# Seven products instead of eight for five of eight k-pairs of an MLP's up-projection, token-major, with the residual stream in DRAM

## The chip, the cores and the metric

The kernel runs on one core of one Trainium2 chip. The metric is the device time of one execution in microseconds, the median over several runs. The core has a matmul engine (TensorE, PE in the profile, with its weight loads as PEld), a vector engine (VectorE, DVE), an activation engine (ScalarE, ACT), a general engine (GpSimd, POOL) and a sync engine (SyncE, SP) that here only issues transfers. Operands lie in SBUF, matmul results in PSUM, which has eight banks of 128 x 512 fp32; weights, inputs and outputs lie in DRAM.

## The reference

Two layers over 256 tokens of width 2048, all in fp32. Each layer is a mixer (layer 0: gated short convolution and chunked attention; layer 1: two gated linear recurrences) and an MLP, each between two RMS norms and added to the stream h. Cut to what matters here:

```python
for l in range(DEPTH):                       # 2
    g = norm_g[l]
    u = rmsnorm(h, g[0])
    y = mixer_l(u) @ w_out[l]                # w_out 2048 x 2048
    h = h + rmsnorm(y, g[1])
    u = rmsnorm(h, g[2])
    z = jnp.square(jax.nn.relu(u @ mlp_w1[l])) @ mlp_w2[l]   # 2048 -> 8192 -> 2048
    h = h + rmsnorm(z, g[3])
```

## The kernel before

**Precision.** TensorE multiplies in a reduced fp32 format (F32R). To get fp32 accuracy, every operand is split into a high part (ScalarE's cast, `whi`, L222) and a residual (VectorE's subtraction, `wlo`, L223), and a product is three matmuls: high x high, high x residual, residual x high.

**Weights.** A *slab* is two k-tiles of 128 rows by 512 columns (512 KB). SyncE's queue brings it into one of 7 raw tiles, ScalarE and VectorE convert it into one of 6 pairs of tiles `whi`, `wlo`, TensorE uses it. Each weight is used once, by both token tiles (two times 128 tokens).

**Forms of a block of 512 output columns.** `Block` (L235 to L237) is token-major: for each token tile 128 columns of x are the stationary operand and the weights stream through, 512 at a time; a slab is 12 matmuls. `UpBlock` (L271, L274) is feature-major: 128 columns of weights are stationary and x streams through, 512 columns wide (both parts of both token tiles) for the high weights and 256 wide for the residual; a slab is 8 + 8 matmuls. Its result already has hidden features on partitions, as the next product needs it.

**The MLP.** The hidden width 8192 is cut into 8 chunks of 1024. `mlp` runs up(0), then for c = 1 to 7 up(c) and down(c-1), then down(7). An up chunk is 16 slabs: two `UpBlock`s of 512 columns, only the first block of chunk 0 is a `Block`. Its evacuation (L452 to L462) joins the halves, squares the ReLU and splits the result into `hid[c]`. A down chunk is 4 `Block`s of 4 slabs, added into `y` (L476).

**What sets the order.** The program is written slab by slab (`run`), and a scheduler lays the instructions of each engine out in one fixed order; each engine then works through its order and waits on semaphores. Weight conversions are placed some slabs ahead, as far as the tiles allow. The last four slabs of the out-projection and of the MLP are done for the first token tile, then for the second, with the norm between (`tail`, `between`); the next phase then begins with 6 slabs for the first token tile only (`lead`). `later` puts an action off by a number of slabs.

**The stream.** h (two tiles of 128 x 2048) and y stay in SBUF through the out-projection and the MLP; h goes to DRAM (`hsave`) only for layer 1's mixer. x is loaded into h at the start, and the sums of squares are taken from there.

Of the kernel before, what the change touches and what calls it, by code (L numbers as in the profile page):

```python
# [11 lines left out]
F32 = mybir.dt.float32  # L12
# [15 lines left out]
X_BUFS = 1  # L28
# [11 lines left out]
def trunk(ctx, tc, x, x_t, norm_g, ng_cols, e_win, rbf, e_wout, o_win, lbraw, smalls, wa2, ba, o_wout, w1, w2,  # L40
# [160 lines left out]

    class Block:
# [7 lines left out]
        def load(self, s, extra=None):  # L210
            k0 = self.kts[s * SLAB]
            raw = rawp.tile([P, SLAB, 512], F32, name="raw")
            pool, tag, bufs = (wp, "w", W_BUFS) if extra is None else (extra, "x", X_BUFS)
            hi = pool.tile([P, SLAB, 512], F32R, name=tag + "hi", bufs=bufs)
            lo = pool.tile([P, SLAB, 512], F32R, name=tag + "lo", bufs=bufs)
# [66 lines left out]

    def banks():
        return [accp.tile([P, 512], F32, name="acc") if j % 2 == 0 else aux() for j in range(4)]
# [34 lines left out]
    def run(blocks, tail=0, between=None, extra=None, rate=0.0, hooks={}, lead=None):  # L319
# [24 lines left out]
        for t in range(NT):  # L344
            for i, (b, s) in enumerate(items[n:]):
                if t == 0:
                    b.load(s, extra if i < X_BUFS else None)
                b.mm(s, t)
            if between is not None and t == 0:
                between(0)  # L350
# [34 lines left out]
    def gbc_tile(pool, l, i):  # L385
        t = pool.tile([P, D], F32, name="gbc", bufs=1)

        def load(c):
            def f():
                cs = slice(c * 1024, (c + 1) * 1024)  # L390
                nc.sync.dma_start(out=t[:, cs], in_=norm_g[l, i, cs].partition_broadcast(P))
            return f
        return t, [load(0), load(1)]


    def out_proj(l, w, kts, X2, y, h, X, ypool, reload=()):
        gbc, gl = gbc_tile(ypool, l, 1)
        hooks = {2: gl[0:1], 5: gl[1:2]}
        for i, f in enumerate(reload):
            hooks[9 + 2 * i] = [f]  # L400
# [11 lines left out]
        def between(t):  # L412
            add_post(t, y, rsqrt_of(total(ss[t]), 1, 1.0 / D), h)
            rst[t] = prenorm(t, h[t], l, 2, X, ypool)

        run([Block(wview(w), nb * 512, 512, kts if nb == 0 else ALLK, X2.get, mk(nb)) for nb in range(4)],
            tail=TAIL, between=between, extra=ypool, hooks=hooks)
        return rst, lambda: between(1)

    def mlp(l, X, rst, y, ypool, between, lead):  # L420
        gbc, gl = gbc_tile(ypool, l, 3)
# [7 lines left out]
        def finish(t):  # L429
            between(t, rsqrt_of(sl[t], 1, None, base[t]))  # L430
# [6 lines left out]
        def up(c):  # L437
            def mk(j):
                def evac(t, ps):
                    r = ypool.tile([P, 512], F32, name="relu", bufs=2)  # L440
                    nc.scalar.activation(out=r, in_=ps, func=AF.Relu)
                    r2 = ypool.tile([P, 512], F32, name="ulo", bufs=2)
# [4 lines left out]
            def mk_up(j):  # L447
                st2 = {}

                def evac(i, ps):  # L450
                    a = ypool.tile([P, 256], F32, name="ulo", bufs=2)
                    nc.scalar.copy(out=a, in_=ps[:, 256:512])  # L452
                    if i % 2 == 0:
                        st2["z"] = ypool.tile([P, 2, 256], F32, name="relu", bufs=2)
                    z = st2["z"]
                    nc.vector.tensor_tensor(out=z[:, i % 2, :], in0=ps[:, 0:256], in1=a, op=ALU.add)  # L456
                    if i % 2:
                        r2 = ypool.tile([P, 2, 256], F32, name="relu2", bufs=1)
                        nc.vector.scalar_tensor_tensor(out=r2, in0=z, scalar=0.0, in1=z, op0=ALU.max, op1=ALU.mult)
                        hi, lo = pair(x2p, "x2", 2, 256)  # L460
                        nc.scalar.copy(out=hi, in_=r2)
                        nc.vector.tensor_tensor(out=lo, in0=r2, in1=hi, op=ALU.subtract)  # L462
                        hid[c].put2(c * 8 + j * 4 + i - 1, hi, lo)
                return evac
            hid[c] = Hid()
            return [Block(w1v, (c * 2 + j) * 512, 512, ALLK, X.get, mk(j)) if c == 0 and j == 0 else
# [604 lines left out]
```

## Time and profile before

| | |
|---|---|
| median of 3 runs | 2280.32 us (2279.87 to 2280.66) |
| the profiled execution | 2280.16 us |
| its span in the trace | 2278.2 us |
| PE, PEld busy | 2262.2 us, 1915.0 us |
| DVE, ACT, POOL busy | 1415.3 us, 1089.8 us, 15.2 us |
| read from HBM, written | 424.28 MB, 4.20 MB |
| mean granted clock of TensorE | 0.998 |

Busy time is the time in which an engine had at least one instruction running; matmuls overlap, so a busy TensorE need not be at its peak. In a group row stand line, engine, operation, result <- inputs, shapes and count, then busy us and mean ns of one, then the idle time before them and what ended it. In a timeline row stand start, duration, engine, line and operation, and in brackets the idle time just before and what ended it.

### The profile page before, as it was taken

The page shows a single profiled execution, that of the slowest core. Times are in us where ns is not written, and L with a number is a line of the kernel's source. Part 1 is how long each engine was busy: PE and PEld are TensorE (multiplying, and loading weights), DVE is VectorE, ACT ScalarE, POOL GpSimd, SP SyncE. Part 2 cuts the span into 40 slices and gives each one's busy share as a digit, 9 for nine tenths or more (in the row PEclk, how much of TensorE's full clock was granted, in tenths as well). Part 3 has the DMA queues.
Part 4 walks back from the last instruction along what each step waited for, and adds up shares of the span by engine and source line. Part 5 has one row for each costly group of instructions (what it writes and reads, how often), then busy time and mean ns, then how long its engine had stood idle before and what let it go on. Part 6 is the DMA issues. An engine that isn't in the chain of part 4 may idle for free.

```text
span 2278.2 us, 29937 instructions
## 1 busy us (share of the span) xinstructions
PE 2262.2 (99%) x11486; PEld 1915.0 (84%) x11486; DVE 1415.3 (62%) x1856; ACT 1089.8 (48%) x1550; POOL 15.2 (1%) x30
## 2 busy tenths in 40 slices
PE   9999999999999999999999999999999999999998
PEld 7888888888888888888888888888888888888886
DVE  6656656655565665656877767657556565556556
ACT  7444445544444444444746454546444444444443
POOL 0000000000000000000000000000000000000000
PEclk9999999999999999999999999999999999999999
DMA  9555565655655656656655445475565665665652
GB/s 345 167 177 174 168 229 176 206 188 189 194 188 192 193 187 192 192 187 203 213 174 167 153 144 159 166 257 185 186 193 187 193 193 185 192 191 191 194 187 100
DMA packets 219390, 430.43 MB, mean 189 GB/s; under 512 B 13392, under 2 KB 14192, under 8 KB 218992
## 3 DMA queue, kind: packets, MB, share of 16 engines
q1 hardware_dynamic: 217152, 422.63, 58.0%
q0 software_dynamic: 1376, 4.79, 0.7%
q8 instruction: 90, 1.47, 0.3%
q10 hardware_dynamic: 720, 1.11, 0.1%
q14 instruction: 52, 0.43, 0.1%
HBM read 424.28 MB, written 4.20 MB: 188 GB/s over the span
## 4 chain that ended last, share of the span: by engine, by line
PE 97%; ACT 1%; DVE 1%; DMA 1%; issue 0%; SPq 0%; DVEq 0%; ACTq 0%
PE aux L274 23%; PE acc L235 18%; PE acc L236 18%; PE acc L237 18%; PE aux L271 12%; PE acc L274 3%; PE acc L271 2%; PE aux L815 1%; PE aux L175 1%; DMA h<-x 1%; PE aux L862 0%; ACT junk L362 0%; DVE wlo L223 0%; PE aux L700 0%; DMA raw<-e_win 0%
## 5 line engine op out<-in xcount | busy, mean ns | idle before, releaser
L223 DVE TENSOR_TENSOR wlo<-raw,whi 128x1024 fp32r<-128x1024 f32 (+1 forms) x781 | 952.9, 1223 | 760.7 <-ACT whi L222 759.3
L222 ACT CAST whi<-raw 128x1024 fp32r<-128x1024 f32 (+1 forms) x781 | 821.5, 1054 | 1029.9 <-PE acc L237 590.0
L274 PE MATMUL aux<-xt,whi 128*128 128x512 f32 x2240 | 590.4, 393 | 0.0
L235 PE MATMUL acc<-whi,x 128*128 128x512 f32 x1264 | 492.7, 390 | 0.0
L236 PE MATMUL acc<-wlo,x 128*128 128x512 f32 x1264 | 492.3, 389 | 0.0
L237 PE MATMUL acc<-whi,x 128*128 128x512 f32 x1264 | 492.0, 389 | 0.0
L274 PEld LDWEIGHTS aux<-xt,whi 128*128 128x128 f32 x2240 | 401.8, 189 | 75.5 <-DVE relu L456 4.2
L271 PE MATMUL aux<-xt,wlo 128*128 128x256 f32 x2240 | 339.4, 282 | 0.0
L271 PEld LDWEIGHTS aux<-xt,wlo 128*128 128x128 f32 x2240 | 317.8, 190 | 23.1
L237 PEld LDWEIGHTS acc<-whi,x 128*128 128x128 f32 x1264 | 237.3, 188 | 49.3
L235 PEld LDWEIGHTS acc<-whi,x 128*128 128x128 f32 x1264 | 237.3, 188 | 48.7
L236 PEld LDWEIGHTS acc<-wlo,x 128*128 128x128 f32 x1264 | 237.3, 188 | 48.5
L235 PE MATMUL acc<-whi,xt 128*128 128x512 f32 x576 | 227.8, 398 | 1.8 <-ACT xt L522 1.5
L236 PE MATMUL acc<-wlo,xt 128*128 128x512 f32 x576 | 225.5, 392 | 1.9 <-DVE wlo L223 1.8
L237 PE MATMUL acc<-whi,xt 128*128 128x512 f32 x576 | 225.2, 391 | 0.0
L236 PEld LDWEIGHTS acc<-wlo,xt 128*128 128x128 f32 x576 | 108.3, 188 | 25.4 <-DVE wlo L223 4.3
L235 PEld LDWEIGHTS acc<-whi,xt 128*128 128x128 f32 x576 | 108.0, 188 | 24.6 <-ACT xt L522 2.0
L237 PEld LDWEIGHTS acc<-whi,xt 128*128 128x128 f32 x576 | 108.1, 188 | 22.8 <-issue 0.3
L274 PE MATMUL acc<-xt,whi 128*128 128x512 f32 x320 | 101.5, 398 | 0.0
L271 PE MATMUL acc<-xt,wlo 128*128 128x256 f32 x320 | 63.9, 281 | 0.0
L271 PEld LDWEIGHTS acc<-xt,wlo 128*128 128x128 f32 x320 | 55.6, 189 | 7.2
L476 DVE TENSOR_TENSOR y<-acc,y 128x512 f32<-128x512 f32 x96 | 61.5, 682 | 0.0
(204 smaller groups left out, 1073.7 us busy)
## 6 DMA issues: line engine op xcount, KB each, us to landing
raw<-w SPq DMA_DIRECT2D x512, 512.0 KB, 3.7
raw<-o_win SPq DMA_DIRECT2D x112, 512.0 KB, 3.7
raw<-e_win SPq DMA_DIRECT2D x95, 512.0 KB, 4.2
raw<-e_wout SPq DMA_DIRECT2D x32, 512.0 KB, 4.4
raw<-o_wout SPq DMA_DIRECT2D x32, 512.0 KB, 3.7
gbc<-norm_g SPq DMA_DIRECT2D x8, 512.0 KB, 6.6
h<-x SPq DMA_DIRECT2D x4, 512.0 KB, 12.0
hsave<-h POOLq DMA_DIRECT2D x2, 1024.0 KB, 4.8
```

The costliest lines, as they stand in the source:

```text
L175: nc.tensor.transpose(out=ps[:, k * P:(k + 1) * P], in_=src[:, k * P:(k + 1) * P], identity=ident)
L222: nc.scalar.copy(out=hi[:, a:b, n], in_=raw[:, a:b, n])
L223: nc.vector.tensor_tensor(out=lo[:, a:b, n], in0=raw[:, a:b, n], in1=hi[:, a:b, n], op=ALU.subtract)
L235: nc.tensor.matmul(ps, xh, hi[:, i, 0:self.n], start=first, stop=False)
L236: nc.tensor.matmul(ps, xh, lo[:, i, 0:self.n], start=False, stop=False)
L237: nc.tensor.matmul(ps, xl, hi[:, i, 0:self.n], start=False, stop=last)
L271: nc.tensor.matmul(self.ps[j][:, 0:NT * P], lo[:, i, cs], x[:, 0, :], start=False, stop=last and i == SLAB - 1)
L274: nc.tensor.matmul(self.ps[j], hi[:, i, cs], x, start=s == 0 and i == 0, stop=False)
L476: nc.vector.tensor_tensor(out=y[t][:, cs], in0=ps, in1=y[t][:, cs], op=ALU.add)
L815: nc.tensor.matmul(ps[0:m, u * 64:(u + 1) * 64].rearrange("p (b n) -> p b n", n=wd), K[:, u * P:u * P + m], Q[:, us].rearrange("p (b two n ...
```

## The change

**Pairs.** For chunks 1 to 7 both column halves (L and R, 512 columns each) of an up chunk are computed together, token-major, by `Pairs`, in 8 slabs of one k-pair (two k-tiles by 1024 columns: two raw tiles). For a k-pair the token tiles (a, b), the two k-tiles and the column halves make a 2 x 2 by 2 x 2 block product. `PAIRS = "CSCSSCSS"`: the three C pairs do it plainly, by 8 products (24 matmuls); the five S pairs by 7 products of block sums (21 matmuls), in a form of Strassen's and Winograd's. The sums of x (`Differences`) are made once a layer, the sums of weights in place in the raw tiles. Products of all pairs accumulate in 8 banks (`p2`, `bR`, `p1`; `q3`, `q4`, `q5`, `p6`, `p7`), all PSUM has, and are put together once, behind the last pair (`comb`). A C slab takes two converted tile pairs, an S slab four.

**Token-major results.** The 4 blocks of 128 x 512 are squared, then transposed on TensorE (four 128 x 128 each) and split, some slabs into the following down chunk. Chunk 0 is now two `Block`s, with transposes too.

**The stream.** h now lies in 4 KB half rows (`Row`) in a pool of 7 that it shares with the norm's gains, `Differences` and the scratch U. After the out-projection's norm it is stored to `mid` in DRAM by GpSimd's queue, and read back in the last chunk. In layer 0 the out-projection reads x again; at the start x passes through raw tiles for its sums of squares only. The extra weight tile of the tail (`X_BUFS`) goes. The last output's pieces are 512, 512, 512, 256, 256 columns instead of 256, 512, 512, 512, 256.

```diff
-X_BUFS = 1
+PAIRS = "CSCSSCSS"
...
+    class Differences:
+        def make(self, tmp):
+            p = self.p
+            x = self.X.full[p // 2][:, 2 * (p % 2):2 * (p % 2) + 2, :, :]
+            xf = tmp().rearrange("p (k n) -> p k n", k=2)
+            nc.vector.tensor_tensor(out=xf, in0=x[:, :, 0, :], in1=x[:, :, 1, :], op=ALU.add)
+            a, b = slice(0, P), slice(P, 2 * P)
+            sf = tmp().rearrange("p (i n) -> p i n", i=4)
+            for i, (u, v, op) in enumerate(((xf[:, 0, b], xf[:, 1, b], ALU.subtract),
+                                            (sf[:, 0, :], xf[:, 0, a], ALU.subtract),
+                                            (xf[:, 0, a], xf[:, 0, b], ALU.subtract),
+                                            (sf[:, 1, :], xf[:, 1, a], ALU.add))):
+                nc.vector.tensor_tensor(out=sf[:, i, :], in0=u, in1=v, op=op)
+            o = self.pool.tile([P, 2, 4, P], F32R, name="s")
+            self.hi, self.lo = o[:, 0], o[:, 1]
+            nc.scalar.copy(out=self.hi, in_=sf)
+            nc.vector.tensor_tensor(out=self.lo, in0=sf, in1=self.hi, op=ALU.subtract)
...
+    class Pairs:
+        def load(self, s):
+            raws = [rawp.tile([P, SLAB, 512], F32, name="raw") for _ in range(2)]
+            for raw, n in zip(raws, (self.n0, self.n0 + 512)):
+                nc.sync.dma_start(out=raw, in_=self.wv[:, 2 * s:2 * s + 2, n:n + 512])
+
+            def conv(raw, i=slice(0, SLAB)):
+                hi, lo = w_pair()
+                nc.scalar.copy(out=hi[:, i, :], in_=raw[:, i, :])
+                nc.vector.tensor_tensor(out=lo[:, i, :], in0=raw[:, i, :], in1=hi[:, i, :], op=ALU.subtract)
+                return hi, lo
...
+            L, R = raws
+            if PAIRS[s] == "C":
+                self.w[s] = [conv(L), conv(R)]
+                return
+            plain = conv(L)
+            r1 = conv(R, slice(1, 2))
+            add(R[:, 1, :], R[:, 1, :], R[:, 0, :])
+            add(R[:, 0, :], R[:, 0, :], L[:, 0, :])
+            two = conv(R)
+            add(L[:, 0, :], L[:, 0, :], R[:, 1, :])
+            add(L[:, 1, :], L[:, 1, :], L[:, 0, :])
+            self.w[s] = [plain, r1, two, conv(L)]
+
+        def product(self, n, s, x, w, i):
...
+            nc.tensor.matmul(ps, xh, hi[:, i, :], start=first, stop=False)
+            nc.tensor.matmul(ps, xh, lo[:, i, :], start=False, stop=False)
+            nc.tensor.matmul(ps, xl, hi[:, i, :], start=False, stop=done and not (n == "bR" and i == 0))
+
+        def mm(self, s, t):
...
+            if PAIRS[s] == "C":
+                for n, t, j in (("p2", 0, 0), ("bR", 1, 1), ("q4", 1, 0), ("q3", 0, 1)):
+                    for i in range(2):
+                        self.product(n, s, x[t][i], w[j], i)
+                if "C" not in PAIRS[s + 1:]:
+                    nc.scalar.copy(out=self.U[3], in_=z.pop("bR"))
+                return
...
+            self.product("p1", s, x[0][0], L, 0)
+            if end:
+                nc.scalar.copy(out=s1, in_=z["p1"])
+            self.product("p2", s, x[0][1], L, 1)
+            if end:
+                comb("aL", z["p2"], s1, ALU.add)
+                self.evac(0, 0, out["aL"])
+            self.product("q3", s, d.get(3), r1, 1)
+            self.product("q5", s, d.get(0), two, 0)
+            self.product("p7", s, d.get(2), two, 1)
+            self.product("p6", s, d.get(1), four, 0)
+            if end:
+                nc.vector.tensor_tensor(out=u, in0=z["p6"], in1=s1, op=ALU.add)
+                nc.vector.tensor_tensor(out=u3, in0=z["p7"], in1=u, op=ALU.add)
+            self.product("q4", s, x[1][1], four, 1)
+            if end:
+                comb("aR", z["q5"], u, ALU.subtract)
+                comb("aR", z["q3"], out["aR"], ALU.add)
+                self.evac(0, 1, out["aR"])
+                comb("bL", z["q4"], u3, ALU.add)
+                self.evac(1, 0, out["bL"])
+                comb("bR", z["q5"], u3, ALU.subtract)
+                comb("bR", zb, out["bR"], ALU.add)
+                self.evac(1, 1, out["bR"])
...
-            return [Block(w1v, (c * 2 + j) * 512, 512, ALLK, X.get, mk(j)) if c == 0 and j == 0 else
-                    UpBlock(w1v, (c * 2 + j) * 512, 512, ALLK, X.both, mk_up(j)) for j in range(2)]
+            if c == 0:
+                return [Block(w1v, j * 512, 512, ALLK, X.get, mk(j)) for j in range(2)]
+            n = [0]
+
+            def evac(t, j, z):
+                nc.vector.scalar_tensor_tensor(out=z, in0=z, scalar=0.0, in1=z, op0=ALU.max, op1=ALU.mult)
+                n[0] += 1
+                later(lambda: hid[c].put(t, c * 2 + j, split4(x2p, "x2", transpose4(z))), 2 + 2 * n[0])
+            evac.tile = lambda: ypool.tile([P, 512], F32, name="ulo", bufs=4)
+            return [Pairs(w1v, c * 1024, X, diffs, U, evac)]
...
+        work = [lambda p=p: difference(p) for p in range(len(PAIRS)) if PAIRS[p] == "S"]
+        run(up(0), lead=lead_in, hooks={LEAD + 1 + 2 * i: [f] for i, f in enumerate(work)})
+        scratch()
...
     def load_x(t, i):
-        c = slice(i * 1024, (i + 1) * 1024)
-        nc.sync.dma_start(out=h[t][:, c], in_=x[t * P:(t + 1) * P, c])
+        xp = raw_tile()
+        nc.sync.dma_start(out=xp.rearrange("p a b -> p (a b)"), in_=x[t * P:(t + 1) * P, i * 1024:(i + 1) * 1024])
+        for k in range(2):
+            junk = mp.tile([P, 512], F32, name="junk", bufs=1)
+            nc.scalar.activation(out=junk, in_=xp[:, k, :], func=AF.Square,
+                                 accum_out=xss[t][:, 2 * i + k:2 * i + k + 1])
```

**How the order moves.** Line numbers below are those of the kernel named. First VectorE before, at the turn from an up chunk (the last tiles of `UpBlock`) to the down chunk:

```order
L223 TENSOR_TENSOR wlo_5166<-raw_5164,whi_5165 128x1024
L456 TENSOR_TENSOR relu_5056<-aux_4890,ulo_5054 128x256
L456 TENSOR_TENSOR relu_5056<-aux_4891,ulo_5060 128x256
L459 SCALAR_TENSOR_TENSOR relu2_5063<-relu_5056 128x512
L223 TENSOR_TENSOR wlo_5186<-raw_5184,whi_5185 128x1024
L462 TENSOR_TENSOR x2_5065<-relu2_5063,x2_5065 128x512
L456 TENSOR_TENSOR relu_5076<-aux_4892,ulo_5074 128x256
L456 TENSOR_TENSOR relu_5076<-aux_4893,ulo_5080 128x256
L459 SCALAR_TENSOR_TENSOR relu2_5083<-relu_5076 128x512
L223 TENSOR_TENSOR wlo_5204<-raw_5202,whi_5203 128x1024
```

There the evacuation stands between conversions that are five slabs ahead of TensorE. VectorE in the changed kernel for one S slab (L332 residuals, L336 sums of raw weights in place):

```order
L332 TENSOR_TENSOR wlo_4739<-raw_4734,whi_4738 128x1024
L332 TENSOR_TENSOR wlo_4743<-raw_4735,whi_4742 128x512
L336 TENSOR_TENSOR raw_4735<-raw_4735 128x512
L336 TENSOR_TENSOR raw_4735<-raw_4735,raw_4734 128x512
L336 TENSOR_TENSOR raw_4734<-raw_4734,raw_4735 128x512
L336 TENSOR_TENSOR raw_4734<-raw_4734 128x512
L332 TENSOR_TENSOR wlo_4749<-raw_4735,whi_4748 128x1024
L332 TENSOR_TENSOR wlo_4755<-raw_4734,whi_4754 128x1024
```

Eight operations stand where two conversions stood; the scheduler has put all four sums ahead of the third residual. VectorE in the changed kernel behind an up chunk's last pair (L224 down tiles, L383, L397, L398 combinations, L598 squarings):

```order
L224 TENSOR_TENSOR wlo_5055<-raw_5053,whi_5054 128x1024
L598 SCALAR_TENSOR_TENSOR ulo_5022<-ulo_5022 128x512
L397 TENSOR_TENSOR s_3981<-aux_4776,s_3981 128x512
L224 TENSOR_TENSOR wlo_5075<-raw_5073,whi_5074 128x1024
L398 TENSOR_TENSOR s_3982<-aux_4772,s_3981 128x512
L383 TENSOR_TENSOR ulo_5042<-aux_4768,s_3981 128x512
L383 TENSOR_TENSOR ulo_5046<-aux_4720,s_3982 128x512
L383 TENSOR_TENSOR ulo_5042<-aux_4727,ulo_5042 128x512
L598 SCALAR_TENSOR_TENSOR ulo_5046<-ulo_5046 128x512
L598 SCALAR_TENSOR_TENSOR ulo_5042<-ulo_5042 128x512
L383 TENSOR_TENSOR ulo_5049<-aux_4768,s_3982 128x512
L224 TENSOR_TENSOR wlo_5093<-raw_5091,whi_5092 128x1024
```

Seven combinations and squarings now stand between the second and the third down tile (`wlo_5075`, `wlo_5093`); one more combination stands ahead of the first. On TensorE the transposes (L175) of the first three blocks come just before the third down slab's residual matmuls.

181 lines of the change are left out of this document (102 added, 79 removed).

## The prediction

> **What bounds the kernel now.** I read the page's busy rows first, then the chain that ended last, then who made TensorE wait.
>
> ```profile
> span 2278.2 us, 29937 instructions
> PE 2262.2 (99%) x11486; PEld 1915.0 (84%) x11486; DVE 1415.3 (62%) x1856; ACT 1089.8 (48%) x1550; POOL 15.2 (1%) x30
> PEclk9999999999999999999999999999999999999999
> PE 97%; ACT 1%; DVE 1%; DMA 1%; issue 0%; SPq 0%; DVEq 0%; ACTq 0%
> PE acc L236 <- DVE wlo L223: 1.8, 4, 0.5
> PE acc L235 <- ACT xt L522: 1.5, 1, 1.5
> ```
>
> TensorE (PE) is busy for 99% of the span at full granted clock, 97% of the chain is its own work, and its two largest waits are 1.8 and 1.5 us. Nothing is late; the time is the sum of matmuls. A busy share does not say what one matmul costs, because they overlap, so I take distances between starts in the timeline: the same matmul of two consecutive down slabs, and the first matmul of two consecutive up slabs.
>
> ```profile
> 599.90 0.39 PE L235 MATMUL acc<-whi,x 128*128 128x512 f32 x1
> 602.62 0.39 PE L235 MATMUL acc<-whi,x 128*128 128x512 f32 x1
> ...
> 614.98 2.00 PE L274 MATMUL aux<-xt,whi 128*128 128x512 f32 x8
> 617.78 2.00 PE L274 MATMUL aux<-xt,whi 128*128 128x512 f32 x8
> ```
>
> A down slab holds 12 matmuls of 512 columns: 602.62 - 599.90 = 2.72 us, 0.2267 each (the listed 0.39 is one matmul's latency). An up slab holds 8 of 512 and 8 of 256 columns, 12 equivalents, and takes 2.80: 3% dearer. From the chain, one whole cycle of an up chunk and a down chunk:
>
> ```profile
> 1871.88 1.81 PE aux L274 x8
> ...
> 1960.23 1.81 PE aux L274 x8
> ```
>
> That is 88.35 us, 14 of them in the program. The stretches of that cycle, up then down (us, then busy of PE, PEld, DVE, ACT, POOL, clock, DMA share, GB/s):
>
> ```profile
> 1871.90:1916.20 44.30, 44.30 (x254) 38.73 (x254) 25.05 (x28) 19.57 (x24) 0.00 (x0) 1.00 0.59 190
> 1916.20:1960.20 44.00, 44.00 (x198) 36.49 (x197) 26.83 (x30) 18.56 (x20) 0.00 (x0) 1.00 0.62 191
> ```
>
> VectorE (DVE) has 36 us spare per cycle, ScalarE (ACT) 50. Those are what the change spends.
>
> **The change, part by part.**
>
> *Matmuls in the up chunk.* Three plain pairs take 24 matmuls of 512 columns each, five summed pairs 7 x 3 = 21: 177 x 0.2267 = 40.1 us. The down chunk keeps 192 x 0.2267 = 43.5.
>
> *Transposes added.* Token-major results must be turned: 4 blocks x 4 transposes per cycle. The trace has such groups of four between matmuls:
>
> ```profile
> 1346.62 0.40 PE L237 MATMUL acc<-whi,xt 128*128 128x512 f32 x1
> 1346.86 0.60 PE L175 MATMUL aux<-ident,tmp 128*128 128x128 f32 x4
> 1347.22 0.48 PE L235 MATMUL acc<-whi,xt 128*128 128x512 f32 x1
> 1347.53 0.40 PE L236 MATMUL acc<-wlo,xt 128*128 128x512 f32 x1
> ```
>
> From 1346.86 to 1347.53 is 0.67 with one matmul in it: 0.45 per four, 1.8 per cycle. TensorE's work is then 40.1 + 43.5 + 1.8 = 85.4, against 88.35.
>
> *VectorE in the up chunk.* This decides what is left of those 2.9 us. Rows by shape, and starts of neighbours:
>
> ```profile
> L223 DVE TENSOR_TENSOR wlo<-raw,whi 128x1024 fp32r<-128x1024 f32 x779 | 951.5, 1224 | 755.7 <-ACT whi L222 754.4
> L222 ACT CAST whi<-raw 128x1024 fp32r<-128x1024 f32 x779 | 820.3, 1055 | 1026.5 <-PE acc L237 590.0 <-PE aux L274 430.3 <-DMA raw<-e_win 2.0
> L476 DVE TENSOR_TENSOR y<-acc,y 128x512 f32<-128x512 f32 x96 | 61.5, 682 | 0.0
> L831 DVE TENSOR_TENSOR x<-x,prods 128x512 f32<-128x512 f32 x30 | 19.4, 685 | 0.0
> ...
> 1207.84 3.48 DVE L223 TENSOR_TENSOR wlo<-raw,whi 128x1024 fp32r<-128x1024 f32 x3
> ...
> 1146.85 0.69 DVE L894 TENSOR_TENSOR tmp<-tmp 128x512 f32<-128x512 f32 x1
> 1147.58 0.69 DVE L896 SCALAR_TENSOR_TENSOR tmp<-tmp 128x512 f32<-128x512 f32 x1
> ```
>
> Three residual subtractions in a row take 3.48, not 3 x 1.224 = 3.67: neighbours that do not need each other start 1.13 apart. Two where the second reads the first start 0.73 apart. In-place sums of raw weights are not in the trace; the nearest row is L831, in place on 512 columns, 0.685. A plain pair needs two subtractions, 2.3 us, against 5.44 of matmuls. A summed pair needs three of 1.224, one of half that width (0.685) and four sums of 0.685 in a chain: 7.1, less about 0.2 of overlap: 6.9, against 21 x 0.2267 = 4.76 of matmuls. So VectorE loses 2.1 us in each summed pair and gains 3.1 in each plain one. ScalarE has 3 x 1.055 and a half cast there, 3.8: not the bound; each cast that needs a sum runs under VectorE's next two operations (1.4 against 1.06).
>
> The lead that VectorE can hold is set by the six converted pairs of tiles:
>
> ```profile
> 603.76 0.39 PE L237 MATMUL acc<-whi,x 128*128 128x512 f32 x1
> 604.18 1.05 ACT L222 CAST whi<-raw 128x1024 fp32r<-128x1024 f32 x1 [1.67 <-PE acc L237]
> 605.27 1.23 DVE L223 TENSOR_TENSOR wlo<-raw,whi 128x1024 fp32r<-128x1024 f32 x1 [1.50 <-ACT whi L222]
> ```
>
> A tile freed at 604.15 is full again at 606.50, 2.35 later. Counting from the first matmul of an up chunk (lead = first use of a slab's first tile minus its completion): slab 2's first tile takes the slot of slab 0's first, free after 18 matmuls (4.1), full at 6.6, used at 10.2: lead 3.6. Slab 3's takes slab 1's first, free at 7.0, full at 9.3, used at 15.6: lead 6.3. From there VectorE runs without rest: slab 4, 6.3 - 2.1 = 4.2; slab 5, 2.1; slab 6 (behind a plain one), 5.2; slab 7, 3.1. Inside a summed slab the third tile is the tight one (made 4.5 after the first, used 9 matmuls = 2.0 after it): 0.6 left in slab 7. So the up chunk just goes through without waiting, and ends with the lead used up.
>
> *The turn to the down chunk.* Between slab 7's last tile and the third down tile VectorE has 13 operations: three subtractions of 1.22 and ten of about 0.685 (eight combinations and squarings that read PSUM or scratch). That is 10.5, some 9.5 with the overlaps. TensorE's work in that stretch is 33 matmuls (six of slab 7, two down slabs, three high parts of the third), 7.5, and three groups of transposes, 1.35; the last tile's lead adds about 0.4 (the ledger gives 0.7, casts that wait for slots take some): 9.2. That leaves 0.3, and I add as much for the transposes, which stand in front of the third slab's residual matmuls and wait for their own squarings: a wait of 0.6; bounds 0, and 3.0 (first rival). After that the down chunk's spare (1.2 of each 2.72) refills the lead. One cycle: 85.4 + 0.6 = 86.05; saved 2.3; times 14, **-32.2 us**.
>
> *Behind the wait.* Queued on VectorE behind the combinations are down tiles 3 and 4 and the split of the new hidden block; the latter is needed a whole chunk later, so only TensorE's next slab waits.
>
> The Trainium skill, "VectorE: DVE Perf Modes", section "The DRAIN you can't avoid", says that a Vector operation does not start until the pipeline of the one before is empty, with or without semaphores. The row of three subtractions in 3.48 speaks against it for operations that do not depend on each other, and its own section on two instructions without a wait allows an earlier start. Were it to hold throughout, the result would be the first rival's.
>
> *First chunk of each layer.* The second block of chunk 0 goes to the token-major form too: 8 slabs at 2.72 instead of 2.80 save 0.6, eight transposes cost 0.9. It now needs accumulation banks that the squared-ReLU of the block before must first empty, and that ScalarE instruction stands behind casts of 1.05 each; the five sets of token differences (about 2.6 of VectorE each) also run there, under slabs in which VectorE is idle for 1.5 of 2.72. Bounds 0 and 4 us a layer; I take 2. With the 0.3 above, **+4.6** for both.
>
> *The stream in DRAM.*
>
> ```profile
> raw<-w SPq DMA_DIRECT2D x512, 512.0 KB, 3.7
> h<-x SPq DMA_DIRECT2D x4, 512.0 KB, 12.0
> ```
>
> Stores and reloads go out many slabs before use on queues whose engines are 60% busy; a weight slab lands 3.7 after issue and seven raw tiles (3.5 slabs, 15 us) lie ahead even though summed pairs hold theirs longer. At the start x now passes through the seven raw tiles, with landings of 12 us, so fewer weights are in flight while the first block already waits now and then. The tail loses one spare weight tile. Bounds 0 and 6; I take **+2**. The last output chain keeps its five pieces a tile: 0.
>
> Sum, on the profiled execution's 2280.16: 2280.2 - 32.2 + 4.6 + 2 = 2254.6; with those small waits more likely understated than not I say **2256 us**. The profiled execution lies 0.16 under the median shown, 2280.32, which changes nothing.
>
> **Rivals.**
>
> *VectorE becomes the bound (slower or no gain).* If a summed pair costs VectorE 7.2 instead of 6.9 (no overlap, 0.03 per dependent sum) and a plain one 2.45, the leads after slab 3 run 6.3, 3.9, 1.5, 4.5, 2.0, and are about 1 us short at the end; the turn takes the full 10.5 against 8.8, nearly 2 more. Together 3.0 a cycle: 88.4, no saving, and with +6.6 from the other terms 2287. It decides from about 5% more VectorE time per summed pair. For it: the ledger ends at zero. Against it: the row of 3.48. Halfway (2.5% more) costs 1.2 a cycle: 2273.
>
> *No wait at the turn.* The interleaved transposes and a little more overlap cover it: 85.4 a cycle, 2254.6 - 8 = 2246, and 2242 if the first chunks are smooth. For it: 0.6 is small against ten operations.
>
> *The clock answers to the waits.* If waits that come every 86 us took the granted clock down for even 5% of the matmul time, some 100 us of it would run slower.
>
> ```profile
> 2200.00:2278.00 78.00, 68.82 (x304) 56.66 (x302) 46.67 (x65) 27.76 (x40) 0.00 (x0) 0.95 0.37 124
> ```
>
> Only the stretch with the 9 us of idle end shows 0.95; short waits do not. At 0.95 throughout the time would be 2256 x 1.05, about 2370. The Trainium skill, "TensorE: Matmul & The Clock Gate", section "What's actually happening", ties the fall to an idle window of about 3.4 us; no wait forecast here is that long.
>
> **How the numbers follow.** About 0.2% (4.6 us) is what a measurement can tell from no change. Forecast (2248 to 2268): 0.56. No wait at the turn, below 2248: 0.19. VectorE bound: 0.24, of which 0.08 lands at 2268 to 2275, 0.07 within 0.2% of before, 0.09 slower. Clock: 0.01, slower. So faster 0.83, same 0.07, slower 0.10. The range 2242 to 2276 leaves out 0.05 below and 0.16 above.
>
> **What would show it.** In the changed profile: a cycle, from one up chunk's first matmul to the next, of 86.0 (85.4 and 88.4 for the rivals); matmuls still 0.2267 apart inside summed pairs; TensorE's waits headed by VectorE's down-chunk subtraction (L224) and combinations (L383), some 0.6 per cycle, and almost none on the pair residuals (L332); VectorE near 90% busy. If L332 heads the waits, VectorE is the bound; waits on raw weights or on ScalarE's casts would be a mechanism that I have not priced.

## The result and the profile after

The changed kernel takes 2261.61 us (median of four, 2261.25 to 2261.99); the kernel before took 2280.45 on the same chip. The ratio is 0.9918, 95% interval 0.9901 to 0.9935: faster by 18.8 us. The prediction said 2256 in a range of 2242 to 2276. The profiled execution took 2261.99.

From the profile page of the changed kernel, then three rows of its list of TensorE's waits (us in total, how often, the longest):

```profile
span 2260.2 us, 28830 instructions
PE 2238.3 (99%) x10556; PEld 1850.9 (82%) x10556; DVE 1750.7 (77%) x2328; ACT 1173.7 (52%) x1612; POOL 20.7 (1%) x40
PE 75%; DVE 14%; issue 5%; ACT 4%; DMA 1%; ACTq 0%; DVEq 0%; SPq 0%
```

```profile
PE acc L237 <- DVE wlo L224: 3.7, 9, 1.2
PE aux L175 <- DVE s L509: 2.2, 3, 1.3
...
PE aux L358 <- DVE wlo L332: 0.2, 1, 0.2
```

In this and the other timelines and lists here, `...` marks rows left out. These views disagree. By busy time and by the waits TensorE looks as full as before: 99% busy, and its largest wait is 3.7 us in all. By the chain of waits something has changed: TensorE's own work is 75% of the chain, where it was 97%, and VectorE carries 14%. The distances between starts decide which view is right. One cycle, from the first matmul of one up chunk to the first of the next (timeline of TensorE: start, us, engine, line, operation):

```profile
608.03 0.39 PE L357 MATMUL acc<-whi,xt 128*128 128x512 f32 x1
...
645.43 0.39 PE L357 MATMUL aux<-whi,s 128*128 128x512 f32 x1
645.95 0.50 PE L358 MATMUL aux<-wlo,s 128*128 128x512 f32 x1
646.28 0.39 PE L359 MATMUL aux<-whi,s 128*128 128x512 f32 x1
...
648.59 0.39 PE L236 MATMUL acc<-whi,x 128*128 128x512 f32 x1
648.97 0.50 PE L237 MATMUL acc<-wlo,x 128*128 128x512 f32 x1
649.30 0.40 PE L238 MATMUL acc<-whi,x 128*128 128x512 f32 x1
...
655.44 1.04 PE L175 MATMUL aux<-ident,ulo 128*128 128x128 f32 x8
656.63 0.50 PE L237 MATMUL acc<-wlo,x 128*128 128x512 f32 x1 [0.15 <-DVE wlo L224]
...
694.68 0.39 PE L357 MATMUL acc<-whi,xt 128*128 128x512 f32 x1
```

The cycle is 694.68 - 608.03 = 86.65 us, where it was 88.35 and 86.05 was forecast. Elsewhere in it matmuls start 0.227 apart, but the residual matmul at 645.95, in the last pair of the chunk, comes 0.52 behind the one before it. No wait is printed there: a matmul's latency is 0.39, so a stop of up to 0.16 beyond the usual 0.227 is counted as busy time, and the 0.13 that is left of this one is not printed. The same happens at the first down slab (648.97, distance 0.38), and at 656.63 in the third one, behind the transposes, a wait of 0.15 is printed. The matmul after a stop is late again: 646.28 and 649.30 come 0.33 behind, not 0.227. Against the same places without a stop (e5 below) the cycle loses 0.40 in the last pair, 0.27 at the first down slab and 0.42 at the third: 1.09 together.

VectorE ahead of slab 4, through the last two summed pairs and in the turn to the down chunk, and the busy times of that cycle's up and down chunks and of one summed pair (stretch, its us, then busy of PE, PEld, DVE, ACT, POOL, granted clock, DMA share, GB/s):

```profile
623.64 1.83 DVE L332 TENSOR_TENSOR wlo<-raw,whi 128x1024 fp32r<-128x1024 f32 x2 [0.32 <-ACT whi L331]
...
634.84 2.87 DVE L336 TENSOR_TENSOR raw<-raw 128x512 f32<-128x512 f32 x4
637.63 4.22 DVE L332 TENSOR_TENSOR wlo<-raw,whi 128x1024 fp32r<-128x1024 f32 x4
641.88 2.87 DVE L336 TENSOR_TENSOR raw<-raw 128x512 f32<-128x512 f32 x4
644.67 2.51 DVE L332 TENSOR_TENSOR wlo<-raw,whi 128x1024 fp32r<-128x1024 f32 x2
647.10 0.68 DVE L383 TENSOR_TENSOR ulo<-acc,s 128x512 f32<-128x512 f32 x1
...
655.36 1.21 DVE L224 TENSOR_TENSOR wlo<-raw,whi 128x1024 fp32r<-128x1024 f32 x1
```

```profile
608.03:648.58 40.55, 40.42 (x178) 33.14 (x177) 36.33 (x42) 22.72 (x26) 0.00 (x0) 1.00 0.52 165
648.58:694.68 46.10, 45.95 (x209) 37.58 (x208) 38.44 (x46) 20.95 (x23) 0.00 (x0) 1.00 0.67 220
634.84:641.88 7.04, 7.04 (x33) 5.83 (x32) 6.87 (x8) 3.95 (x5) 0.00 (x0) 1.00 0.59 210
```

From the first sum of one summed pair to the first sum of the next VectorE takes 641.88 - 634.84 = 7.04 us, of which it is busy 6.87. TensorE takes 4.76 for the same pair. The four dependent sums cost 2.87 (0.72 apart); the four subtractions, one of them of half the width, 4.22. The same subtractions in the list of groups with shapes kept apart (count, busy us, mean ns, idle time before them):

```profile
L332 DVE TENSOR_TENSOR wlo<-raw,whi 128x1024 fp32r<-128x1024 f32 x294 | 354.5, 1222 | 93.4 <-ACT whi L331 86.6
L332 DVE TENSOR_TENSOR wlo<-raw,whi 128x512 fp32r<-128x512 f32 x70 | 48.0, 686 | 12.8 <-ACT whi L331 12.8
```

Fourteen cycles of 88.36 - 86.66 = 1.70 us make -23.8; the profiled time fell by 2280.16 - 2261.99 = 18.2, so 5.6 us came back outside the cycles. Two questions are open: what the cycle still waits for, and where the 5.6 went.

### The profile page after: what moved, and what is told of

Read it like the earlier page. It is cut to its first block, busy times and chain, and to the rows that moved or that the text cites. A ratio compares the mean times of both kernels' runs of the same rounds, so it can differ in the third digit from the quotient of the medians.

```text
span 2260.2 us, 28830 instructions
## 1 busy us (share of the span) xinstructions
PE 2238.3 (99%) x10556; PEld 1850.9 (82%) x10556; DVE 1750.7 (77%) x2328; ACT 1173.7 (52%) x1612; POOL 20.7 (1%) x40
## 4 chain that ended last, share of the span: by engine, by line
PE 75%; DVE 14%; issue 5%; ACT 4%; DMA 1%; ACTq 0%; DVEq 0%; SPq 0%
PE acc L237 18%; PE acc L238 17%; PE acc L236 17%; DVE raw L336 4%; DVE wlo L332 4%; PE acc L275 3%; PE aux L275 3%; ACT whi L331 3%; DVE wlo L224 2%; PE aux L272 2%; PE acc L272 2%; DVE ulo L383 2%; PE aux L359 2%; PE aux L357 2%; PE aux L358 2%
## 5 line engine op out<-in xcount | busy, mean ns | idle before, releaser
L224 DVE TENSOR_TENSOR wlo<-raw,whi 128x1024 fp32r<-128x1024 f32 (+1 forms) x561 | 676.2, 1219 | 303.9 <-ACT whi L223 301.9
L223 ACT CAST whi<-raw 128x1024 fp32r<-128x1024 f32 (+1 forms) x561 | 582.5, 1053 | 587.1 <-PE acc L238 464.7
L331 ACT CAST whi<-raw 128x1024 fp32r<-128x1024 f32 x364 | 343.5, 969 | 372.3 <-DVE raw L336 213.8
L332 DVE TENSOR_TENSOR wlo<-raw,whi 128x1024 fp32r<-128x1024 f32 x364 | 397.9, 1119 | 106.2 <-ACT whi L331 99.4
L236 PE MATMUL acc<-whi,xt 128*128 128x512 f32 x640 | 254.1, 399 | 0.5 <-ACT xt L671 0.5
L237 PE MATMUL acc<-wlo,xt 128*128 128x512 f32 x640 | 251.6, 394 | 3.0 <-DVE wlo L224 3.0
L238 PE MATMUL acc<-whi,xt 128*128 128x512 f32 x640 | 250.8, 392 | 0.0
L336 DVE TENSOR_TENSOR raw<-raw 128x512 f32<-128x512 f32 x280 | 193.8, 692 | 9.3
L236 PEld LDWEIGHTS acc<-whi,xt 128*128 128x128 f32 x640 | 120.6, 189 | 25.7 <-ACT xt L671 1.4
L238 PEld LDWEIGHTS acc<-whi,xt 128*128 128x128 f32 x640 | 120.5, 188 | 25.3 <-issue 0.3
L357 PE MATMUL acc<-whi,xt 128*128 128x512 f32 x308 | 120.0, 390 | 0.0
L359 PE MATMUL acc<-whi,xt 128*128 128x512 f32 x308 | 119.8, 389 | 0.0
L358 PE MATMUL acc<-wlo,xt 128*128 128x512 f32 x308 | 119.8, 389 | 0.0
L358 PE MATMUL aux<-wlo,s 128*128 128x512 f32 x280 | 110.6, 395 | 1.9 <-DVE wlo L332 0.2
L357 PE MATMUL aux<-whi,s 128*128 128x512 f32 x280 | 109.2, 390 | 0.0
```

Of the source, the lines that this page charges most:

```text
L223: nc.scalar.copy(out=hi[:, a:b, n], in_=raw[:, a:b, n])
L224: nc.vector.tensor_tensor(out=lo[:, a:b, n], in0=raw[:, a:b, n], in1=hi[:, a:b, n], op=ALU.subtract)
L236: nc.tensor.matmul(ps, xh, hi[:, i, 0:self.n], start=first, stop=False)
L237: nc.tensor.matmul(ps, xh, lo[:, i, 0:self.n], start=False, stop=False)
L238: nc.tensor.matmul(ps, xl, hi[:, i, 0:self.n], start=False, stop=last)
L331: nc.scalar.copy(out=hi[:, i, :], in_=raw[:, i, :])
```

## The experiments

My theory was that VectorE's backlog in summed pairs, which is not made up again before the turn, makes the cycle's waits. The rivals: the six converted tile pairs set when a slab is ready whatever VectorE's load; or the token-major form costs it by itself, in its switches between transposes and matmuls and in its turn. Cycles below are distances between first matmuls of up chunks, as above.

### e1: without the four sums

```
             def add(dst, a, b):
-                nc.vector.tensor_tensor(out=dst, in0=a, in1=b, op=ALU.add)
+                pass
```

> The four sums of the weights in each of the five summed pairs are left out, so those pairs multiply plain weights and the product is another one; every product, transpose, conversion and transfer stays. Mine (VectorE's backlog makes the waits): 2.9 us less of VectorE per summed pair, 14 a cycle; the 0.9 us of waits in a cycle go, cycle 85.7, time about 2248. Rival (the six converted tile pairs set when a slab is ready, not VectorE's time): cycle stays at 86.6, time 2261. Rival (the matmuls themselves cost more than their count, in the switches between transposes and products): cycle stays at 86.6 too.

Measured 2245.80 us (ratio 0.985, 0.9835 to 0.9864); cycle 40.12 + 45.44 = 85.56. With the same matmuls, casts, slots and turn, 1.1 us a cycle went when 14 us of VectorE's work a cycle went. Slots alone and the form alone are out. The run takes away the sums' time and the links that they are in the chain of a pair together; e6 below bears on which of the two counts.

### e2 and e3: four summed pairs, and one

```
-PAIRS = "CSCSSCSS"
+PAIRS = "CSCSCSCS"    (e2)
+PAIRS = "CCCCCCCS"    (e3)
```

> Four summed pairs instead of five, plain and summed in turn: three matmuls more per cycle (0.7 us), VectorE 4.7 us less work per cycle. Mine: 180 + 192 matmuls by 0.2267 are 84.3, transposes 2.1, and no waits: cycle 86.4, time 2258, three faster than the change in spite of the added matmuls. Rival (the token-major form's own turn costs the waits, whatever the pairs): 86.66 + 0.68 = 87.3 a cycle, time 2271.

> One summed pair, the last; seven plain. 12 matmuls more per cycle than the change. Mine: 189 + 192 matmuls by 0.2267 are 86.4, transposes 2.1, no waits: cycle 88.4, time about 2286, so a little slower than before: the form without its saving costs the transposes less the three matmuls. Rival (the form costs more than its transposes): 86.66 + 2.72 = 89.4 a cycle, time 2300.

Measured 2255.71 us (0.9893, 0.9876 to 0.9909) with cycle 40.80 + 45.44 = 86.24, and 2283.99 us (1.0016, 1.0007 to 1.0026) with 42.84 + 45.44 = 88.28. The up chunks are their matmuls and nothing else: 180 x 0.2267 = 40.81 and 189 x 0.2267 = 42.85. One of e3's ten executions took 5144.09 us; the record gives no reason, and the median is the same without it. So four summed pairs beat five by 5.9 us with three matmuls more per chunk. The form without the saving costs the same per cycle as before (88.28 against 88.36), and what makes e3 slower lies outside the cycles.

### e4, e7 and e10: converted and raw tiles

```
-RAW_BUFS = 7        (e4, e7)
+RAW_BUFS = 6
-W_BUFS = 6          (e4, e10)
+W_BUFS = 7
```

In e10 the room for the seventh converted pair comes from elsewhere: the combinations' second sum is written over the first product, and the output of the squares, which nothing reads, has two bytes an element.

> One more pair of converted weight tiles (7 for 6) and one less raw tile (6 for 7), which is what fits. The matmuls' work is the same. Mine (VectorE's backlog, with a longer lead ahead of it): the lead that is used up at the turn is one slab longer, 0.6 to 0.9 us less a cycle, and at the three junctions the seventh pair stands where the spare tail tile stood, 2 us more: 2247 to 2253. Rival (VectorE's rate alone, no lead helps since it never gets ahead): cycle 86.6, time 2261.

> Six raw tiles for seven, and the six converted pairs as in the change: the half of the run with seven converted pairs that takes something away. Mine: raw tiles are not what the chunks wait for, cycle 86.7; the run with seven converted pairs lost 6 us between the two MLPs against the change, and if the missing raw tile is its cause this run loses them too: about 2266; the 1.5 us that it won at the first junction are not won here. Rival (fewer raw tiles keep the conversions from running ahead and the order of VectorE's work is the better for it): cycle 85.6 and a time near 2253.

> The change's own order of pairs (CSCSSCSS) with seven converted pairs, and seven raw tiles as in the change: one thing altered where the fourth run altered two. Mine: cycle 85.6 as in the fourth run, nothing lost between the MLPs, the junctions as in the ninth: about 2242 to 2243. Rival (six raw tiles helped in the fourth run): cycle above 86 and 2250 or more.

Measured: e4 2253.62 us (0.988, 0.9865 to 0.9895), e7 2267.72 (0.9947, 0.9933 to 0.9962), e10 2243.53 (0.984, 0.9826 to 0.9853). In e4 and e10 most cycles are 85.57, a few up to 1.4 longer in the down chunk; in e7 the up chunk is as in the change (40.56) and the down chunk 46.0 to 47.3 instead of 46.1. The time of e4 lies just above the 2247 to 2253 that I expected; it has the stop told below. One more converted pair therefore removes nearly all of the wait, and one raw tile less costs 6 us. I had expected the raw tile to cost something between the MLPs only; the down chunks pay too. That a longer lead helps does not contradict e1: the backlog is finite, since plain pairs and the down chunk work it off, so either less of it or more room ahead of it is enough.

Between the MLPs the runs with six raw tiles have a stop that the others have not. A row of TensorE's waits in e7, and the stretch around the stop:

```profile
PE aux L175 <- issue: 4.1, 2, 2.8
```

```profile
1110.00:1130.00 20.00, 17.24 (x72) 13.82 (x71) 15.76 (x24) 11.88 (x17) 2.46 (x6) 0.91 0.86 275
```

A stop of 2.8 us goes with a granted clock of 0.91 over its 20 us; in the next 20 it is 1.00. In e4 the stop is 3.6 us and the clock 0.97 and 0.94 in the stretches of 20 us from 1100. What released the transposes there the trace doesn't say ("issue"), and no run was spent on it: it stays open.

### e5: the same five summed pairs in another order

```
-PAIRS = "CSCSSCSS"
+PAIRS = "SCSCSSCS"
```

> The same five summed pairs in another order: the first pair of a chunk is summed, the second plain (SCSCSSCS for CSCSSCSS); three summed pairs stand behind the middle as before, but two of them no longer end the chunk one after the other. No instruction more or less in a cycle. With one summed pair less, and with a seventh converted pair, the cycle was 85.57 us worked back to five pairs (40.12 up, 45.45 down), and this is what 372 - 3 matmuls and the transposes cost without a wait. Mine (the backlog of VectorE at the chunk's end): with a plain pair between the last summed ones the lead is not used up; cycle 85.6, 14 x 1.09 = 15 us less than the change: 2246. Rival (any order has the same backlog over a chunk, and five pairs need the seventh tile pair): cycle 86.6, time 2261.

Measured 2246.65 us (0.9853, 0.9839 to 0.9868). No instruction of a cycle is added or taken away, and the time falls by 15.0. From its page, two rows of its waits, and one cycle:

```profile
span 2244.8 us, 28817 instructions
PE 2226.1 (99%) x10556; PEld 1851.8 (82%) x10556; DVE 1749.4 (78%) x2328; ACT 1172.1 (52%) x1612; POOL 20.6 (1%) x40
PE 96%; DVE 2%; DMA 1%; ACT 1%; issue 0%; DVEq 0%; SPq 0%; ACTq 0%
```

```profile
PE aux L175 <- DVE s L509: 2.2, 3, 1.3
PE acc L237 <- DVE wlo L224: 2.1, 4, 0.6
```

```profile
605.46 0.39 PE L357 MATMUL acc<-whi,xt 128*128 128x512 f32 x1
691.03 0.39 PE L357 MATMUL acc<-whi,xt 128*128 128x512 f32 x1
```

The cycle is 85.57, that of e1. The list of waits fell by some 2 us only, with the time down by 15; the rest came out of TensorE's "busy" time, 2238.3 to 2226.1 for the same 10556 instructions. The chain of waits had it right: TensorE's own share is back at 96%. VectorE is as loaded as before (78%), so its load over a chunk is not the bound. What counts is where the summed pairs stand: with a plain pair between the last ones the lead is not used up at the turn.

### e6: two of the four sums on GpSimd

```
-            add(L[:, 0, :], L[:, 0, :], R[:, 1, :])
-            add(L[:, 1, :], L[:, 1, :], L[:, 0, :])
+            add(L[:, 0, :], L[:, 0, :], R[:, 1, :], nc.gpsimd)
+            add(L[:, 1, :], L[:, 1, :], L[:, 0, :], nc.gpsimd)
```

> In each summed pair the two sums into the left raw tile go to GpSimd, 70 adds x 2 in the program; the other two stay on VectorE. Mine (VectorE's time makes the waits): a summed pair takes 1.4 us less of VectorE, 7 us a cycle; if an add of 128x512 takes GpSimd no more than about 2 us, the waits go: cycle 85.6, time 2246. Rival (the two engines disturb each other, or GpSimd's adds are so slow that the fourth conversion comes later than now): VectorE's own instructions in these pairs longer than 0.69 and 1.12 us, cycle above 86.7, time above 2262.

Measured 2385.38 us (1.0462, 1.0444 to 1.0479); the cycles take 94.7 to 97.1. The time is the rival's, and of its reasons the later fourth conversion does most. Groups by line and operation (count, busy us, mean ns, idle time before them) of the changed kernel and of e6, and the timeline of e6 over two summed pairs in a row:

```profile
L332 DVE TENSOR_TENSOR wlo<-raw,whi 128x1024 fp32r<-128x1024 f32 x364 | 397.9, 1119 | 106.2 <-ACT whi L331 99.4
L336 DVE TENSOR_TENSOR raw<-raw 128x512 f32<-128x512 f32 x280 | 193.8, 692 | 9.3
```

```profile
L332 DVE TENSOR_TENSOR wlo<-raw,whi 128x1024 fp32r<-128x1024 f32 x364 | 404.4, 1140 | 306.5 <-ACT whi L331 302.9
L336 POOL TENSOR_TENSOR raw<-raw 128x512 f32<-128x512 f32 x140 | 242.2, 1730 | 1066.0 <-DVE raw L336 992.1 <-ACT s L304 68.4
L336 DVE TENSOR_TENSOR raw<-raw 128x512 f32<-128x512 f32 x140 | 96.8, 692 | 4.6
```

```profile
656.82 1.42 DVE L336 TENSOR_TENSOR raw<-raw 128x512 f32<-128x512 f32 x2
659.43 1.32 DVE L332 TENSOR_TENSOR wlo<-raw,whi 128x1024 fp32r<-128x1024 f32 x1 [1.19 <-ACT whi L331]
663.01 2.96 DVE L332 TENSOR_TENSOR wlo<-raw,whi 128x1024 fp32r<-128x1024 f32 x3 [2.26 <-ACT whi L331]
666.00 1.42 DVE L336 TENSOR_TENSOR raw<-raw 128x512 f32<-128x512 f32 x2
...
658.37 1.30 POOL L336 TENSOR_TENSOR raw<-raw 128x512 f32<-128x512 f32 x1 [7.93 <-DVE raw L336]
659.75 2.15 POOL L336 TENSOR_TENSOR raw<-raw 128x512 f32<-128x512 f32 x1
...
661.93 2.52 ACT L331 CAST whi<-raw 128x1024 fp32r<-128x1024 f32 x3 [2.05 <-POOL raw L336]
```

An add takes GpSimd 1.73 us in the mean, inside the "about 2" that I had set: the first of a pair 1.30, the second 2.15. VectorE's sums take 692 ns as they did, but none of them runs beside a GpSimd add. One subtraction of each pair does, and it takes 1.32 in the row shown instead of 1.22 (over all subtractions, both shapes together, that makes 1140 ns against 1119). So the engines do disturb each other a little. How much of the second add's 0.85 above the first is that can't be told, since every second add has a subtraction beside it; two first adds of the run that have VectorE at work beside them nearly throughout take 1.72 and 1.79. A summed pair now takes 666.00 - 656.82 = 9.18 us instead of 7.04, with VectorE idle 1.19 and 2.26 in it; with both adds at 1.30 it would still be some 8.3, by my estimate from these rows. The pair is a chain across three engines: two sums, two GpSimd adds (3.53 from 658.37 on), the cast, the subtraction. ScalarE takes its casts in order, so the next pair's plain cast stands behind the one that waits for GpSimd, and VectorE's next subtraction behind that. My expectation counted VectorE's instructions and left out that on in-order engines a longer link holds up the next pair as well. For the theory this is a limit: what sets the pace of a summed pair is its chain. In the changed kernel the chain is nearly all VectorE (6.87 of 7.04 busy), and that is why VectorE's time sets it there.

The clock fell too, which it did nowhere in the cycles of the other runs. The mean granted clock of the profiled execution is 0.985. TensorE's longest printed wait in this kernel is 1.3 us, in the pairs 0.9. One place of e6 as two stretches of 3.41 us (columns as in the stretches above):

```profile
934.19:937.60 3.41, 1.86 (x7) 1.01 (x6) 1.82 (x2) 2.89 (x4) 0.48 (x1) 1.00 0.53 154
937.60:941.01 3.41, 3.41 (x9) 2.65 (x8) 3.41 (x4) 1.51 (x3) 0.00 (x0) 0.50 0.77 212
```

Behind 3.41 us in which TensorE was idle for 1.55, in two waits of 0.8, it ran 3.41 us at half the clock. Cycles without such a fall take 94.7, cycles with two of them 95.6 to 95.9. So some 113 of the 124 us that e6 loses against the changed kernel are the longer chain and the disturbance (14 x 8.08), and some 10 the clock, by my estimate.

The Trainium skill, "GPSIMD Engine Reference", section "Elementwise — side-by-side cycle accounting", puts a two-input add on GpSimd at about twice VectorE's time (measured there at 2048 columns); here, at 512 columns, the first add's 1.30 us against 0.692 is 1.9 times, which agrees, and the second's 2.15 is 3.1 times.

### e8: the kernel before without its spare tail tile

```
-X_BUFS = 1
+X_BUFS = 0
```

> The kernel before with one edit: no spare converted tile in the tail of the output projections and of the MLP (X_BUFS 0), as in the changed kernel. Mine (this missing tile makes the later junctions): 1.2 + 2.0 + 1.2 = 4.4 us more, 2284.7. Rival (the junctions cost more in the changed kernel because of the stream's way through DRAM, or of the first pairs of sums): no difference, 2280.3.

Measured 2285.60 us (1.0024, 1.0014 to 1.0033), 5.3 more than the kernel before beside it. TensorE's waits for the sum that ends a projection (L382 in the kernel before), before and in e8, rows of each list in a fence of its own:

```profile
PE aux L175 <- DVE h L382: 0.7, 2, 0.6
```

```profile
PE aux L175 <- DVE h L382: 2.3, 3, 1.3
PE acc L236 <- DVE rs_v L118: 1.2, 1, 1.2
```

In the changed kernel and in e5 the same wait (L509 there) is 2.2 us, three times, at most 1.3. VectorE's order shows it at the first of these junctions: in the kernel before the sum follows the norm's factor at once, in the changed one a conversion stands ahead of the sum (timeline of VectorE, before and after):

```profile
379.62 0.16 DVE L129 SCALAR_TENSOR_TENSOR rs_o<-rs_a,rs_r 128x1 f32<-128x1 f32 x1
379.81 2.74 DVE L382 SCALAR_TENSOR_TENSOR h<-y,rs_o,h 128x512 f32<-128x512 f32 x4
```

```profile
381.18 0.16 DVE L129 SCALAR_TENSOR_TENSOR rs_o<-rs_a,rs_r 128x1 f32<-128x1 f32 x1
381.26 1.22 DVE L224 TENSOR_TENSOR wlo<-raw,whi 128x1024 fp32r<-128x1024 f32 x1
382.40 2.07 DVE L509 SCALAR_TENSOR_TENSOR s<-y,rs_o,s 128x512 f32<-128x512 f32 x3
```

In e8 a subtraction stands there as well (381.63, the sum at 382.77). By stretches the two kernels lose at the same places. Up to the first matmul of the third up chunk (521.07 us before, 522.99 in e8, 521.34 in the changed kernel, which has saved 1.70 by then) e8 loses 1.9 and the changed kernel 2.0; from the last up chunk of layer 0 to the third of layer 1 3.9 and 4.2; behind the last up chunk e8 loses nothing and the changed kernel gains 0.5. So nearly all of the 5.6 us that came back outside the cycles is explained by this one tile: a part of the change that has nothing to do with the products.

### e9: both

The order of e5 and the tiles of e10.

> The order of the fifth run (SCSCSSCS) with seven converted pairs and all seven raw tiles; the room comes from the scratch tile of the combinations (its second sum written over the first product) and a junk tile of two bytes an element that nothing reads. Mine: the cycles stay at 85.57, where nothing waits; at the three junctions, where the missing spare tile cost the kernel before 5.3 us when it was taken away, 4 to 5 us come back: 2242. Rival (the seventh pair doesn't stand for the spare tile, or what was lost between the MLPs with six raw tiles comes from the seventh pair): 2246 to 2250.

Measured 2242.46 us (0.9834, 0.9821 to 0.9848): faster than before by 37.8 us and than the change by 19. The cycles are 40.13 + 45.44 = 85.57, and TensorE's wait for the junction's sum is down:

```profile
PE aux L175 <- DVE s L509: 0.9, 2, 0.5
```

The conversion still stands ahead of the sum at the first junction (380.61 and 381.75 in e9). So that order alone is not what costs the time; with a seventh converted pair TensorE waits less in spite of it. Of the 5.3 us 4.2 came back against e5.

The parts add up over the runs. With 2280.3 for the kernel before, 14 cycles and 5.3 for the missing tile (none of it in e9):

```
run      cycle   2280.3 - 14 x (88.36 - cycle) + 5.3   measured
change   86.66   2261.8                                2261.61
e1       85.56   2246.4                                2245.80
e2       86.24   2255.9                                2255.71
e3       88.28   2284.5                                2283.99
e5       85.57   2246.5                                2246.65
e9       85.57   2241.2 (without the 5.3)              2242.46
```

Two numbers, the cycle and the junctions' tile, carry all of these to within 1.3 us. Of the runs that are not in the table, e10 would be 2241.2 without the 5.3 and took 2243.53, with two of its down chunks 0.5 and 1.4 longer; e4 and e7 have the stop between the MLPs.

## Why the prediction was right, and where it was not

*What bounds the kernel.* Right. TensorE's starts set the time, and matmuls stayed 0.227 apart in summed pairs: three fewer per summed pair is worth 0.68 us each time, as e3 and e2 show (three pairs x 14 x 0.68 = 28.6; measured 2283.99 - 2255.71 = 28.3).

*Matmuls and transposes.* The matmuls of a cycle were 369 x 0.2267 = 83.65, as forecast. Four groups of transposes I put at 1.8; the cycle without a wait (85.57) leaves 1.9. Over fourteen cycles that is some 2 us.

*VectorE in the up chunk.* The mechanism was right and so was nearly the size: a summed pair takes 7.04, where I said 6.9 and the rival 7.2. The rule of the Trainium skill that was weighed there ("VectorE: DVE Perf Modes", "The DRAIN you can't avoid") fell again on the row: three whole subtractions and a half one take 4.22 together, where 3 x 1.222 + 0.686, their means by shape, make 4.35.

*The ledger and the turn.* This is the term that was mis-sized. It gave a wait of 0.6 a cycle, all of it at the turn; the runs without it (e1, e5) put it at 86.66 - 85.57 = 1.09. At the turn itself the size was nearly right: 0.27 at the first down slab and 0.42 at the third, 0.69 together. The other 0.40 lie inside slab 7, where the ledger left 0.6 in hand for the third tile. What failed is its step "From there VectorE runs without rest". The first tile of slab 3 was complete 6.28 ahead of its first use, as the ledger had it (6.3); those of slabs 4 to 7 were 3.56, 1.26, 4.42 and 2.14 ahead, where it had 4.2, 2.1, 5.2 and 3.1. Some 0.6 of the 0.96 that is missing in the end was lost between slabs 3 and 4: VectorE stood idle for 0.32 there, behind a cast that waited for a converted tile to come free (row 623.64), and the summed pair was dearer. The rest was lost in slabs 4 and 6, summed pairs that each cost VectorE more than the 6.9 of the ledger. And a stop between matmuls costs another 0.11 on the next one, which no row had told me. Fourteen times 0.5 is 7 us, nearly the whole miss of the cycles: 32.2 promised, 23.8 found.

*The first chunk of each layer, +4.6.* Wrong as to place. The wait for banks behind casts, 2 us a layer, did not come; the transposes of the second chunk did (their up chunk takes 41.57, the later ones 40.56).

*Stream, start and tail, +2 in bounds of 0 and 6.* The stream in DRAM, the start and the first chunks together cost a net 1.3 us at most, what e9 leaves unexplained in the table, if its seventh pair makes up for the spare tile in full; no run tells the two apart. The spare tail tile costs 5.3 (e8). I had named it and given it less than 2. The two errors cancel, 6.6 forecast and 5.6 found; that the sum came out near is luck in this part.

*The rivals.* VectorE as the bound did not come, but was near: by its price halfway (2.5% more VectorE time per pair) it was 2273, and VectorE took 2% more and lost a quarter of the forecast gain. "No wait at the turn", which I put at 2246 as a rival, is what e5 is, at 2246.65. The clock stayed at 0.999 in the changed kernel. The mechanism of that rival is real all the same. In e6 two waits of 0.8 within 3.41 us were followed by 3.41 us at half the clock, and neither is near the 3.4 us by which I had set the rival aside.

*What would show it.* I wrote that waits would be headed by L224 and L383 and almost none be on L332. The list of waits agrees with that, and it misled: the stop on L332 is 0.40 of the cycle's 1.09, and the list shows 0.2 us of it in the whole program. VectorE was busy for 74.8 of the 86.65 us of that cycle, 86%, where I wrote near 90%. The distance between starts should have been the test that I named.

## What to carry to other kernels

When matmuls overlap, a stop shorter than the latency less the usual distance (0.16 here) is booked as busy time: compare the distance between starts with the same distance in a stretch without waits, and look at the chain of waits, before saying that nothing waits. When an in-order engine falls behind in some steps and catches up in others, alternate the two kinds so that the lead is whole where the dense stretch begins: here the order of eight letters was worth 15 us, four fifths of what the whole change had brought. And a tile that is dropped to make room belongs in the sum as an edit of its own; undo it alone in the old kernel to learn its price.

## What the runs showed of the hardware that I had not expected

- After a stop between matmuls, even one of 0.15 us, the matmul behind the stopped one starts 0.33 us after it instead of 0.227: 0.11 lost once more per stop (645.95 to 646.28, 648.97 to 649.30).
- Eight transposes in a row take 1.04 us, 0.11 from start to start at a latency of 0.27. Four groups of four add some 1.8 to a cycle of e5. In each, three distances of 0.11 and one of 0.03 to the matmul behind it make 0.36, and the next matmul after that one starts 0.31 behind it instead of 0.227.
- A stop of 2.8 us went with a granted clock of 0.91 over the 20 us around it; executions of that kernel at a mean clock of 0.999 took 2267 us and at 0.998 2268 and 2270. The Trainium skill, "TensorE: Matmul & The Clock Gate", section "What's actually happening", ties the fall to an idle window of about 3.4 us; here a printed wait somewhat shorter than that went with it, and in e6 1.55 us of idle in 3.41, in two waits, was enough. An idle window without a break was not needed there.
- A subtraction of 128x1024 that VectorE does beside a GpSimd add of 128x512 takes 1.32 us instead of 1.22, and the add beside it 2.15 where the one before takes 1.30. The longer chain hurt more than this.
